# The first row pair's third outer product by seven inner products, and the second pair's partial results loaded in another order

## The chip, the cores and the metric

The kernel runs on one core of one Trainium2 chip. The metric is the device time of one execution in microseconds (us); lower is better.

## The reference

Soft routing over eight experts: every expert is applied to every token, and the results are added with the softmax of the router's logits as weights.

```
x: [16, 512, 512]   router_logits: [16, 512, 8]   expert_weights: [8, 512, 2048]   (float32)
probs  = softmax(router_logits, axis=-1)
output = sum over e of probs[:, :, e:e+1] * matmul(x, expert_weights[e])      # [16, 512, 2048]
```

For 8192 tokens this is one matrix product: its left factor is x scaled by each expert's probability (8192 rows, 8 x 512 = 4096 deep), its right factor the stacked expert weights (4096 x 2048).

## The kernel before

**Two levels of seven products.** The left factor is cut into 2x2 blocks (even and odd blocks of 256 rows; experts 0 to 3 and 4 to 7) and so is the right factor (the two halves of the experts; the two halves of 1024 columns: B11, B12, B21, B22). The 2x2 block product is done with seven outer products, P1 to P7, in Winograd's form. P1, P5, P2 and P4 come first, each in a stage of its own (`sub_product`), and their results are parked in DRAM tensors, `kept` for P1, P5 and P2, the output itself for P4. Each is split once more in the same way: seven *inner* products of half the size in place of eight. For that, the right factor of an outer product needs four *inner sums*, differences of its four blocks, each one VectorE subtraction over a tile `w` of 128x4096 (`inner_sums`): w5 (`sums[0]`), w6 (`sums[1]`, from w5), w4 (`sums[2]`, from w6) and w7 (`sums[3]`, which overwrites one block).

**The main loop.** The rest goes over 16 row pairs `q` (an even and an odd block of 256 rows each). A pair has four *quarters* (128 rows x 512 columns, `QUARTERS`). For every pair:

1. P6, plain: for each quarter, ScalarE copies the parked P1 (`m1`) into a PSUM bank (L626) and 16 matmuls of 128x512 add to it. VectorE then makes v = bank + parked P5 (`m5`). Between the quarters VectorE also does `c11` (parked P1 + parked P2 makes an output quarter) and `s4` (the left factor of P3), and `a11` for the following pair.
2. P7, plain: 16 more matmuls on each of the four banks. ScalarE copies each result out (`c21`, L664), VectorE adds m5 (`m5 = x + m5`), and GpSimd's queue writes both. VectorE makes the following pair's `s2` between them.
3. P3, whose right factor is B22 (tiles `w3`): in all pairs but the first by seven inner products on 128x512 quarters (`prod`, 7 x 8 matmuls), in the order P1, P2, P5, P6, P3, P7, P4. Inner P5 goes into a bank "q"; VectorE adds this bank to v11 (`r5`); then inner P3 accumulates into the same bank "q". VectorE also adds the bank "x" to v01 after inner P6, before inner P7 accumulates into it.

In the first pair, outer P3 is plain: 4 x 16 matmuls on banks seeded with v by ScalarE (`seeded`, L645), copied out by ScalarE (L681). B22's inner sums are made by VectorE at that time: w5, w6 and w4 during the first pair's P3, and w7, which overwrites a block that the plain P3 reads, in the second pair (`finish(sums)`). `rows.inner()` makes the four left sums of the inner products (VectorE, four operations on 128x8x128).

**What sets the order.** From the main loop on, VectorE and ScalarE work through their instructions in program order (`pinned`). The tile framework places the DMAs of SyncE (all loads of parked results and of x and probabilities) and of GpSimd (the writes of the main loop), and orders matmuls. Parked P1 and P2 tiles and the copied c21 share five buffers in rotation (`share(m=5, ...)`), parked P5 four (`v=4`), v four (`u=4`), r1 and r3 two. A load of a parked tile waits for the buffer's last user: for `m` an earlier output write, or the VectorE and ScalarE operations that read it.

`rows.load_kept(j)` loads the parked P1 and P5 of a quarter; `rows.c11(j)` loads P2 of the quarter and does the addition. `early(j)`, near the end of a pair, loads quarters 0 and 1 of the following pair, and does their `c11` unless it is the first pair's end: then the second pair does them itself, inside its P6.

Of the kernel before, what the change touches and what calls it, by code (L numbers as in the profile page):

```python
# [32 lines left out]
def kernel(  # L33
# [7 lines left out]
    nc = tc.nc  # L41
# [16 lines left out]
    NI = NHQ // 2  # L58
# [60 lines left out]
    act = dve  # L119

    def tt(o, a, b, op):
        dve(nc.vector.tensor_tensor(out=o, in0=a, in1=b, op=op))  # L122
# [15 lines left out]
    def bank():  # L138
        return psum.tile([P, NB], f32, name="ps", tag="ps")

    def mm(ps, z, w, start, stop):
        nc.tensor.matmul(ps, z, w, start=start, stop=stop, skip_group_check=True)  # L142
# [5 lines left out]
    def new_w():  # L148
        return wpool.tile([P, K8, NB], f16, name="w", tag="w")
# [23 lines left out]
    def inner_sums(b, t3=None):  # L173

        t3 = t3 or b[0, 1]
        w = {1: b[0, 0], 2: b[1, 0], 3: b[1, 1], 7: t3}

        def step(p, x, y):
            if p not in w:
                w[p] = new_w()  # L180
            tt(w[p], x, y, SUB)
        return w, [lambda: step(5, b[0, 1], b[0, 0]), lambda: step(6, b[1, 1], w[5]),
                   lambda: step(4, w[6], b[1, 0]), lambda: step(7, b[1, 1], b[0, 1])]

    def inner_weights(b):
        w, sums = inner_sums(b)
        sums[0]()
        yield
        sums[1]()
        sums[2]()  # L190
        yield
        sums[3]()
        return w
# [159 lines left out]
    def half(use="any"):  # L353
        return h_tile([P, NB], f32, use)

    def out_rows(i, odd, u, cols, n):
        return out_f[ds((2 * i + odd) * HQ + u * P, P), ds(cols * NH + n * NB, NB)]
# [72 lines left out]
    def finish(g):  # L430
        try:
            while True:
                next(g)
        except StopIteration as e:
            return e.value
# [6 lines left out]
    for n in range(2):  # L442
# [19 lines left out]
        if n == 0:  # L462
# [3 lines left out]
            w, sums = inner_sums(b11, new_w())  # L466
# [49 lines left out]
    w6, w7, w3 = {}, {}, {}  # L516
# [16 lines left out]
    QUARTERS = ((0, 0), (0, 1), (1, 1), (1, 0))  # L533

    class Rows:
# [57 lines left out]
        def put(self, odd, cols, tn, o, **how):  # L593
            queue = nc.sync if self.q == NI - 1 and not how else nc.gpsimd
            queue.dma_start(out=out_rows(self.q, odd, tn[0], cols, tn[1]), in_=o, **how)  # L595

    rows = Rows(0)
# [5 lines left out]
        rows.c11(j)  # L603
    pinned[0] = True
    o10 = None
    sums = inner_weights(w3)
    for q in range(NI):
        following = Rows(q + 1) if q + 1 < NI else None

        def ahead(make, k, following=following):  # L610
            if following:
                getattr(following, make)(k)

        def plain(ps, r, w, tn, start):
            t, n = tn
            for k in range(2 * K8):
                mm(ps, rows.z[r][k // K8][:, k % K8, ds(t * P, P)], w[k // K8, n][:, k % K8, :],
                   start, k == 2 * K8 - 1)


        xs, vs = [], []
        for j, tn in enumerate(QUARTERS):
            if j > 1:
                rows.load_kept(j)
            x = bank()
            act(nc.scalar.copy(x, rows.m1[tn]))  # L626
            if o10 and j == 0:
                o10()
            if j > 1 or q == 1:
                rows.c11(j)  # L630
            if j < 2:
                rows.s4(j)
            else:
                ahead("a11", j - 2)
            plain(x, 6, w6, tn, False)
            v = half("u")
            tt(v, x, rows.m5[tn], ADD)
            xs.append(x)
            vs.append(v)

        banks = {}

        def seeded(b, v, scale=1.0):
            banks[b] = bank()
            act(nc.scalar.mul(banks[b], v, scale))  # L645
        if q:
            seeded("b", vs[0])
            seeded("d", vs[3], -1.0)
            if q == NI - 1:
                seeded("e", vs[3], -1.0)  # L650
        else:
            seeded(0, vs[0])
            seeded(1, vs[1])


        if q == 1:
            inner3 = finish(sums)
        if q:
            z3 = rows.inner()
        for j, tn in enumerate(QUARTERS):  # L660
            x, m5 = xs[j], rows.m5[tn]
            plain(x, 7, w7, tn, False)
            c21 = half("m")
            act(nc.scalar.copy(c21, x))  # L664
            rows.put(1, 0, tn, c21, accum_op=ADD)
            tt(m5, x, m5, ADD)
            rows.put(1, 1, tn, m5)
            if j < 2:
                ahead("s2", j)


        def early(j):
            if following:
                following.load_kept(j)
                if q:
                    following.c11(j)

        ahead("s3", 0)
        if q == 0:
            def c12(j, tn, rows=rows, vs=vs, banks=banks):  # L680
                act(nc.scalar.copy(vs[j], banks[j]))  # L681
                rows.put(0, 1, tn, vs[j])

            for j, tn in enumerate(QUARTERS):
                plain(banks[j], 3, w3, tn, False)
                if j < 2:
                    seeded(j + 2, vs[j + 2])
                if j < 3:
                    c12(j, tn)
                if j < 2:  # L690
                    early(j)
                    next(sums)
            ahead("s3", 1)
            o10 = lambda: c12(3, QUARTERS[3])
            rows = following
            continue

        def prod(p, b):
            if b not in banks:
                banks[b] = bank()  # L700
            for k in range(K8):
                mm(banks[b], z3[p][:, k, :], inner3[p][:, k, :],
                   p in (1, 5) and k == 0, k == K8 - 1)
            return banks[b]

        def put(j, *args, rows=rows, vs=vs):
            tt(vs[j], *args)
            rows.put(0, 1, QUARTERS[j], vs[j])

        v00, v01, v11, v10 = vs  # L710
        x = prod(1, "x")
        r1 = half("r")
        act(nc.scalar.copy(r1, x))  # L713
        put(0, prod(2, "b"), r1, ADD)
        early(0)
        r5 = prod(5, "q")
        tt(v11, r5, v11, ADD)
        prod(6, "x")
        tt(v01, x, v01, ADD)
        early(1)  # L720
        put(1, prod(3, "q"), v01, ADD)
        prod(7, "x")
        r3 = half("r")
        act(nc.scalar.copy(r3, x))  # L724
        put(2, x, v11, ADD)
        ahead("s3", 1)
        if q < NI - 1:
            d = prod(4, "d")

            def o10(put=put, r3=r3, d=d):  # L730
                put(3, r3, d, SUB)
        rows = following
# [35 lines left out]
```

## Time and profile before

| | |
|---|---|
| median of 7 runs | 1434.1 us (1433.51 to 1436.21) |
| profiled execution: time / span | 1433.43 us / 1431.7 us |
| granted TensorE clock in the span | 1.000 |
| TensorE busy | 1424.8 us (100%), 6654 matmuls |
| VectorE busy | 1032.1 us (72%) |
| ScalarE busy | 271.4 us (19%) |
| GpSimd busy | 220.0 us (15%) |

The span goes from the first instruction's start to the last one's end; the profiled execution's time is 1.7 us longer. In a timeline, each line has a start, a duration, the engine, the source line, the operation, output and inputs, the shape and a count of merged instructions; in brackets stands how long the engine was idle before and what ended that. All VectorE additions and products of the main loop have line L122, all matmuls L142, all SyncE DMAs L133, the writes of outputs L595.

### The profile page before, as it was taken

How to read it: one execution, taken by the hardware profiler on the slowest of the kernel's cores; microseconds unless marked ns; L12 is line 12 of the kernel's file. 1: busy time of each engine (PE TensorE's matmuls, PEld its weight loads, DVE VectorE, ACT ScalarE, POOL GpSimd, SP SyncE). 2: the span in 40 equal slices, each digit the busy share in tenths (PEclk: the TensorE clock that was granted, in tenths of full speed). 3: DMA queues.
4: the chain of work that ended last, by engine and by line, in shares of the span. 5: the costliest groups of instructions: out<-in, count | busy, mean ns of one | idle time of the engine just before them, and what ended most of it. 6: DMA issues, size and time to landing. Idle time of an engine off the chain costs nothing.

```text
span 1431.7 us, 18172 instructions
## 1 busy us (share of the span) xinstructions
PE 1424.8 (100%) x6654; PEld 647.9 (45%) x6654; DVE 1032.1 (72%) x1173; ACT 271.4 (19%) x472; POOL 220.0 (15%) x344
## 2 busy tenths in 40 slices
PE   9999999999999999999999999999999999999998
PEld 4444444444444444444444444444444444444444
DVE  6967585656686867766767687777777877877773
ACT  3211111111111111111111211111111111111111
POOL 3111000110001000001000222222222222222220
PEclk9999999999999999999999999999999999999999
DMA  9899967899649994467866967787777767777764
GB/s 194 190 248 270 269 163 191 181 258 260 208 147 305 352 332 151 132 189 221 215 250 203 300 200 231 235 242 236 228 218 227 214 208 218 226 234 243 220 199 103
DMA packets 192041, 318.92 MB, mean 223 GB/s; under 512 B 51664, under 2 KB 80592, under 8 KB 187344
## 3 DMA queue, kind: packets, MB, share of 16 engines
q1 hardware_dynamic: 135328, 202.92, 44.5%
q0 software_dynamic: 56624, 114.84, 34.1%
q8 instruction: 52, 0.85, 0.2%
q14 instruction: 37, 0.30, 0.1%
HBM read 180.13 MB, written 159.58 MB: 237 GB/s over the span
## 4 chain that ended last, share of the span: by engine, by line
PE 93%; issue 3%; DMA 2%; POOL 1%; DVE 0%; ACT 0%; POOLq 0%; SPq 0%; DVEq 0%; ACTq 0%
PE ps L142 93%; POOL out_dram L595 1%; DMA out_dram<-h 1%; DMA w<-in_expert_weights_dram 0%; DMA h<-kept 0%; POOL w L136 0%; DVE z L122 0%; DVE h L122 0%; ACT ps L626 0%; SPq L133 0%; POOL ident L235 0%; POOLq L595 0%; DVEq L122 0%; POOLq L136 0%; POOLq L235 0%
## 5 line engine op out<-in xcount | busy, mean ns | idle before, releaser
L142 PE MATMUL ps<-w,z 128*128 128x512 f16 x6560 | 1415.2, 379 | 0.8 <-DMA w<-in_expert_weights_dram 0.4
L142 PEld LDWEIGHTS <-z 128*128 128x128 f16 x6560 | 641.6, 98 | 773.2 <-DVE z L122 1.1
L122 DVE TENSOR_TENSOR h<-ps,h 128x512 f32<-128x512 f32 x389 | 267.9, 689 | 313.6 <-PE ps L142 88.8
L122 DVE TENSOR_TENSOR z<-xT,pT 128x2048 f16<-128x2048 f16 x252 | 304.2, 1219 | 31.8 <-PE ps L142 31.2
L122 DVE TENSOR_TENSOR z<-z 128x2048 f16<-128x2048 f16 x280 | 303.6, 1108 | 7.3
L404 ACT COPY h<-ps 128x512 f32<-128x512 f32 x248 | 145.6, 587 | 601.8 <-PE ps L142 594.7
L595 POOL DMA_DIRECT2D out_dram<-h x244 | 154.1, 666 | 532.4 <-DVE h L122 324.7
L122 DVE TENSOR_TENSOR w<-w 128x4096 f16<-128x4096 f16 x36 | 82.3, 2286 | 0.9 <-DMA w<-wd 0.8
L664 ACT COPY h<-ps 128x512 f32<-128x512 f32 x64 | 37.5, 586 | 177.6 <-PE ps L142 176.0
L136 POOL DMA_DIRECT2D h<-in_x_dram x30 | 21.3, 711 | 263.7 <-DMA xT<-h 211.7
L122 DVE TENSOR_TENSOR h<-h,ps 128x512 f32<-128x512 f32 (+1 forms) x78 | 52.7, 676 | 11.0 <-PE ps L142 10.5
L122 DVE TENSOR_TENSOR h<-h 128x512 f32<-128x512 f32 (+1 forms) x67 | 46.0, 686 | 18.8 <-DMA h<-kept 18.7
L136 POOL DMA_DIRECT2D w<-in_expert_weights_dram x41 | 30.7, 763 | 186.4 <-DVE w L161 130.4
L645 ACT ACTIVATE ps<-h 128x512 f32<-128x512 f32 x35 | 21.0, 601 | 168.0 <-DVE h L122 168.0
L626 ACT COPY ps<-h 128x512 f32<-128x512 f32 x64 | 35.5, 592 | 32.6 <-DMA h<-kept 30.4
L136 POOL DMA_DIRECT2D w<-wd x12 | 6.5, 545 | 190.3 <-DVE w L161 116.5
L724 ACT COPY h<-ps 128x512 f32<-128x512 f32 x15 | 8.8, 587 | 120.7 <-PE ps L142 120.7
L713 ACT COPY h<-ps 128x512 f32<-128x512 f32 x15 | 8.8, 587 | 16.4 <-PE ps L142 16.4
L136 POOL DMA_DIRECT2D w<-wdt x8 | 4.4, 555 | 21.9 <-DVE w L161 21.9
L260 DVE CAST z<-ps 128x512 f16<-128x512 f32 x8 | 5.2, 686 | 3.5 <-PE ps L142 3.5
L260 DVE CAST xT<-ps 128x512 f16<-128x512 f32 x4 | 2.6, 687 | 5.4 <-PE ps L142 5.4
L142 PEld LDWEIGHTS <-w 128*128 128x128 f16 x80 | 5.0, 98 | 2.9 <-DMA w<-in_x_dram 1.5
(37 smaller groups left out, 44.2 us busy)
## 6 DMA issues: line engine op xcount, KB each, us to landing
out_dram<-h POOLq DMA_DIRECT2D x244, 256.0 KB, 4.9
kept<-h SPq DMA_DIRECT2D x192, 256.0 KB, 4.4
h<-kept SPq DMA_DIRECT2D x192, 256.0 KB, 4.5
pT<-p_dram SPq DMA_DIRECT2D x124, 256.0 KB, 5.0
w<-in_expert_weights_dram POOLq DMA_DIRECT2D x39, 512.0 KB, 12.9
out_dram<-h SPq DMA_DIRECT2D x75, 256.0 KB, 3.4
xT<-x SPq DMA_DIRECT2D x62, 256.0 KB, 2.9
w<-wd POOLq DMA_DIRECT2D x12, 1024.0 KB, 10.2
```

The lines of the kernel that those rows point to most:

```text
L122: dve(nc.vector.tensor_tensor(out=o, in0=a, in1=b, op=op))
L136: note(nc.gpsimd.dma_start(out=o, in_=i))
L142: nc.tensor.matmul(ps, z, w, start=start, stop=stop, skip_group_check=True)
L260: dve(nc.vector.tensor_copy(o, ps))
L404: nc.scalar.copy(t, ps)
L595: queue.dma_start(out=out_rows(self.q, odd, tn[0], cols, tn[1]), in_=o, **how)
L626: act(nc.scalar.copy(x, rows.m1[tn]))
L645: act(nc.scalar.mul(banks[b], v, scale))
L664: act(nc.scalar.copy(c21, x))
L713: act(nc.scalar.copy(r1, x))
L724: act(nc.scalar.copy(r3, x))
```

## The change

In the first pair, outer P3 is done by seven inner products like in all others. `rows.inner()` and the seeding of banks "b" and "d" are now also done there, and the four inner sums of B22 stand in the first pair: w5 before `rows.inner()`, w6 after the first quarter of P7, w7 after the fourth quarter of P7, w4 after inner P2. The following pair's `s2` parts move from quarters 0 and 1 of P7 to quarters 1 and 2, its first `s3` part from ahead of the inner products to after inner P3. In the second pair, the parked P1 and P5 of quarters 2 and 3 are loaded at the start of P6, ahead of the P2 loads of `c11`.

```diff
-    sums = inner_weights(w3)
+    inner3, sums = inner_sums(w3)
...
-            if j > 1:
+            if j > 1 and q != 1:
                 rows.load_kept(j)
+            if q == 1 and j == 0:
+                rows.load_kept(2)
+                rows.load_kept(3)
...
-        if q:
-            seeded("b", vs[0])
-            seeded("d", vs[3], -1.0)
-            if q == NI - 1:
-                seeded("e", vs[3], -1.0)
-        else:
-            seeded(0, vs[0])
-            seeded(1, vs[1])
+        seeded("b", vs[0])
+        seeded("d", vs[3], -1.0)
+        if q == NI - 1:
+            seeded("e", vs[3], -1.0)
...
-        if q == 1:
-            inner3 = finish(sums)
-        if q:
-            z3 = rows.inner()
+        if q == 0:
+            sums[0]()
+        z3 = rows.inner()
...
-            if j < 2:
-                ahead("s2", j)
+            if q:
+                if j < 2:
+                    ahead("s2", j)
+            elif j < 3:
+                (lambda: sums[1](), lambda: ahead("s2", 0), lambda: ahead("s2", 1))[j]()
...
-        ahead("s3", 0)
-        if q == 0:
-            def c12(j, tn, rows=rows, vs=vs, banks=banks):
-                act(nc.scalar.copy(vs[j], banks[j]))
-                rows.put(0, 1, tn, vs[j])
-
-            for j, tn in enumerate(QUARTERS):
-                plain(banks[j], 3, w3, tn, False)
-                if j < 2:
-                    seeded(j + 2, vs[j + 2])
-                if j < 3:
-                    c12(j, tn)
-                if j < 2:
-                    early(j)
-                    next(sums)
-            ahead("s3", 1)
-            o10 = lambda: c12(3, QUARTERS[3])
-            rows = following
-            continue
+        if q:
+            ahead("s3", 0)
+        else:
+            sums[3]()
...
         put(0, prod(2, "b"), r1, ADD)
         early(0)
+        if q == 0:
+            sums[2]()
         r5 = prod(5, "q")
         tt(v11, r5, v11, ADD)
         prod(6, "x")
         tt(v01, x, v01, ADD)
         early(1)
         put(1, prod(3, "q"), v01, ADD)
+        if q == 0:
+            ahead("s3", 0)
```

## Prediction

> **What bounds the kernel.** I read the page first: busy times and the chain that ended last.
>
> ```profile
> span 1431.7 us, 18172 instructions
> ...
> PE 1424.8 (100%) x6654; PEld 647.9 (45%) x6654; DVE 1032.1 (72%) x1173; ACT 271.4 (19%) x472; POOL 220.0 (15%) x344
> ...
> PE 93%; issue 3%; DMA 2%; POOL 1%; DVE 0%; ACT 0%; POOLq 0%; SPq 0%; DVEq 0%; ACTq 0%
> ```
>
> TensorE is the bound. A matmul less is worth its interval; an operation elsewhere costs nothing until TensorE waits for it. Next, the chain of waits in order of time, around the second pair:
>
> ```profile
> 837.32 4.23 DMA h<-kept
> ...
> 841.63 0.60 ACT ps L626
> 842.23 0.04 issue
> 842.27 585.53 PE ps L142 x2720
> ```
>
> After 842.27 there is no gap: 585.53/2720 = 0.2153 us per matmul. Just before it, the second pair's fourth P6 quarter waited for its parked P1, loaded last. The timeline's line for the weight loads gives the size of this wait:
>
> ```profile
> 842.27 62.69 PEld L142 LDWEIGHTS <-z 128*128 128x128 f16 x291 [0.33 <-issue]
> ```
>
> Without a wait that idle time is 0.215 - 0.097 = 0.12 us, so TensorE lost 0.21 us. These are the places where the change acts. VectorE's timeline there (first pair, end of P6 to P3):
>
> ```profile
> 803.56 0.69 DVE L122 TENSOR_TENSOR h<-h 128x512 f32<-128x512 f32 x1 [4.46 <-DMA h<-kept]
> ...
> 807.67 1.36 DVE L122 TENSOR_TENSOR h<-ps,h 128x512 f32<-128x512 f32 x2
> 808.95 1.22 DVE L122 TENSOR_TENSOR z<-xT,pT 128x2048 f16<-128x2048 f16 x1
> 810.20 1.23 DVE L122 TENSOR_TENSOR z<-z 128x2048 f16<-128x2048 f16 x1
> ...
> 818.75 0.69 DVE L122 TENSOR_TENSOR h<-ps,h 128x512 f32<-128x512 f32 x1 [2.81 <-ACT h L664]
> ...
> 821.75 6.94 DVE L122 TENSOR_TENSOR w<-w 128x4096 f16<-128x4096 f16 x3
> 828.60 1.22 DVE L122 TENSOR_TENSOR z<-xT,pT 128x2048 f16<-128x2048 f16 x1
> ```
>
> VectorE comes late into P7: a parked tile kept it idle until 803.56, and the fourth v is made only at 807.67 (the first of the merged two). ScalarE shows when P7's fourth quarter ended, 818.13:
>
> ```profile
> 818.13 0.59 ACT L664 COPY h<-ps 128x512 f32<-128x512 f32 x1 [2.91 <-PE ps L142]
> ```
>
> **Matmuls.** 64 become 56: 8 x 0.2153 = 1.72 us less. All of it is on the path.
>
> **VectorE, where the gain goes.** The first pair gets the four sums before its inner products need them, four left sums, and six additions. In the order of the changed kernel's instructions, from the fourth v to the r5 addition, each stands behind the one before. Costs are start to start: an addition 0.60 to 0.61 (rows above); a sum 2.19 where the next operation does not read it (2.28 long, the next starts 0.09 before its end); the s2 part of one k 1.25 + 1.15 = 2.40 (808.95, 810.20, and then the next could start at 811.35); the four left sums 2.66, from this row in the second pair, whose successor starts at 851.44:
>
> ```profile
> 848.78 2.74 DVE L122 TENSOR_TENSOR z<-z 128x1024 f16<-128x1024 f16 x4
> ```
>
> 807.67 + v 0.61 + w5 2.19 + left sums 2.66 + m5 0.61 + w6 2.19 + m5 0.60 + s2 2.40 + m5 0.60 + s2 2.40 + m5 0.60 + w7 2.19 + put of P2 0.60 + w4 2.19 = 827.51: r5 starts, ends 0.69 later, 828.20. No other engine holds this chain up: the fourth m5 addition would start at 821.9 (its bank is ready at 818.7) and the P2 addition at 824.7 (P2 is ready at 818.13 + 2 x 1.72 = 821.6). So VectorE is saturated for 20 us.
>
> TensorE does inner P1, P2, P5 and P6 from P7 on without a wait (w5 is there at 810.5, w6 at 816.0): P6's results are seen at 818.13 + 4 x 1.72 = 825.0, and the next matmul could start some 0.2 us before that, at 824.8. Two instructions wait there. In the changed order one inner P4 matmul stands ahead of P3, and it needs w4 (827.6); P3 accumulates into bank "q", so it needs r5 to have read it (828.2). In other pairs r5 costs nothing, since VectorE waits for TensorE, as in the third:
>
> ```profile
> 904.63 0.69 DVE L122 TENSOR_TENSOR h<-ps,h 128x512 f32<-128x512 f32 x1 [0.24 <-PE ps L142]
> ```
>
> With 0.05 us from one engine to the other (ScalarE's end 842.22, matmul 842.27), P3 starts at 828.25 where it could at 824.8: 3.45 us, less the 0.22 of the P4 matmul done in it. **Stall: +3.23 us.** Behind the waiting matmul on TensorE stand P3, P7, P4 and all of the second pair. Its size hangs on the start, 807.67, which DMAs set; I allow 0.8 us either way. P7 needs the x addition, at 828.8, and w7, at 824.8: no further wait.
>
> **B22 itself.** The sums now start at 808.3. Do the blocks land in time?
>
> ```profile
> L136 POOL DMA_DIRECT2D w<-wd x4: 531/536/551, 780.4 to 785.5; - x4
> ...
> DMA to landing us min/median/max: 6.8/10.2/12.5
> ```
>
> At the latest at 785.5 + 12.5 = 798.0; 10 us of cover. Nothing.
>
> **ScalarE, GpSimd, SyncE.** ScalarE loses four seeds and four copies, gains two of each: about 2.4 us less on an engine that is 19% busy. Seed "d" waits for the fourth v (808.36), so the first c21 copy goes from 807.7 to about 809; the m5 additions go later by about 4 us (the first from 808.3 to 813.1), and so do their output writes, and behind them on GpSimd's queue the later c21 writes. These writes free the buffers for the second pair's loads, which issue on SyncE from 814 to 829 and are read by ScalarE from 832 on: hidden.
>
> **The second pair's loads.** All four parked P1 are there by about 829, the seeds come in time, and the 0.21 us wait of before goes: **-0.21 us**. In return the five `m` buffers now hold P1, and the P2 loads of quarters 1 to 3 each wait for the previous quarter's `c11` to free one: addition, issue, landing, addition. VectorE is in order, so s4, the v additions and a11 wait behind each. How long is a landing there?
>
> ```profile
> L133 SPq DMA_DIRECT2D h<-kept x4: 320/320/372, 831.7 to 846.8; - x4
> ...
> DMA to landing us min/median/max: 2.6/3.7/4.4
> ```
>
> The first c11 ends at about 837.5; each following one starts one landing and about 0.8 us after the last. With 3.7 us the fourth starts at 837.6 + 3 x 3.7 + 1.6 = 850.3. From there to the end of the second pair's r5 are 16.6 us of VectorE work by the same prices (a11, v, left sums, four m5, two s2, s3, two additions, r5): 866.9. TensorE, at the second pair's P6 from 833.2 (828.25 + 23 matmuls), would start that inner P3 at 833.2 + 128 x 0.2153 + 32 x 0.2153 = 867.7. Fits, with 0.8 us to spare; landings of 4.0 us would use it up. I take zero; at 4.4 us each (the row's end) it costs about 1.3, at 4.7 about 2.2. Not below zero: nothing there waits in before.
>
> **Clock.** TensorE would stand still for some 3 us with one matmul in between. Nothing in this trace idles it so long after the start; only the first matmuls ran at the slow rate (634 against 379 ns long; nine intervals from 1.3 to 5.1 us are 0.42 each, 0.21 over the normal 0.2153, 1.9 us in all):
>
> ```profile
> L104 PE MATMUL every<-h x10: 531/634/634, 1.3 to 5.1; 128*128 128x512 f16 x10
> ```
>
> So the bounds are 0 and 1.9 us; I take 0, since the page's row of the granted clock has full speed in all slices. [...]
>
> **Sum.** -1.72 + 3.23 - 0.21 = **+1.30 us** on the profiled execution: 1433.43 + 1.30 = 1434.7. The median of the runs is 0.7 us above that execution, so I forecast 1435.4 (+0.09%). A measurement of this kernel can tell about 0.2%, 2.9 us, from no change: this lies within.
>
> **Rivals.**
>
> *No stall (chance 0.12).* If VectorE had the fourth v at about 804.3 (P6's end) in place of 807.67, r5 would end at 824.8 and the whole saving would stay: -1.72 - 0.21 = -1.9, 1432.2 us. Against it: the late parked tiles are loaded before the change begins, by the same queue in the same order. More than 1.93 us can't be gained, so faster by over 0.2% needs a cause that I don't see.
>
> *The P2 loads in series (0.15).* If the landings take more than 4.0 us each, VectorE carries its lateness through the second pair and TensorE waits a second time, at that pair's inner P3. At 4.5 us, the median of all such loads on the page, three landings are 2.4 us longer than at 3.7, 0.8 of which is cover: +1.6, so +2.9 and 1437.0 us; at 4.7, 1437.6. It decides from 4.5 us on. For it: that median. Against it: here they go out one at a time, where the trace's landings are short.
>
> *The clock falls (0.05).* The stall takes it to half, up to +1.9: +3.2, 1437.3 us.
>
> The forecast keeps 0.68. That the change doesn't act can be excluded: the changed order has 8 matmuls fewer.
>
> **Range and chances.** The forecast's own range is 1434.4 to 1436.6 (start of the chain, partial waits in the second pair). With the two slow rivals up to 1437.8, and down to 1432.6, which leaves out the rival without a stall and the outermost cases. Slower by over 0.2%: most of the two slow rivals and little else, 0.17. Faster: 0.02. Within: 0.81.
>
> **What would show it.** In the changed profile: TensorE waits for VectorE (a line w or h) once in the first pair, near 827.6, for about 3 us; VectorE has no idle time from about 804 to 828; the wait at 842 is gone; the second pair's third c11 or fourth shows a wait for DMA, and its r5 does or does not follow TensorE. Wrong if no such stall stands there, if r5 ends by 825, or if the time differs from before by over 2.9 us.

## The result and the profile after

| | before | changed |
|---|---|---|
| median | 1433.79 us (31 runs, 1432.9 to 1438.03) | 1438.42 us (13 runs, 1434.6 to 1440.15) |
| profiled execution: time / span | 1433.43 / 1431.7 us | 1435.12 / 1433.4 us |
| matmuls | 6654 | 6646 |

The ratio is 1.0027, 95% interval [1.0019, 1.0034]: slower by 0.27%, 4.6 us. The forecast was 1435.4 us, in a range of 1432.6 to 1437.8: the direction and the place are as predicted, the size is not. The profiled execution is the second quickest of the 13; other profiles of the changed kernel follow below.

The page of the changed kernel, the lines that answer to those shown of before, and the group of the matmuls:

```profile
span 1433.4 us, 18150 instructions
...
PE 1424.5 (99%) x6646; PEld 647.5 (45%) x6646; DVE 1037.0 (72%) x1183; ACT 268.6 (19%) x468; POOL 219.8 (15%) x344
...
PE 94%; DMA 3%; DVE 2%; issue 0%; SPq 0%; POOL 0%; DVEq 0%; POOLq 0%
...
L142 PE MATMUL ps<-w,z 128*128 128x512 f16 x6552 | 1415.3, 379 | 2.7 <-DVE w L122 1.8
```

Eight matmuls fewer, and yet the busy time of this group is what it was (1415.2 us before): some matmuls took longer. VectorE has come into the chain. TensorE's timeline shows where it waits, first pair, inner P6 to P3:

```profile
814.76 9.88 PE L142 MATMUL ps<-w,z 128*128 128x512 f16 x45
826.45 0.38 PE L142 MATMUL ps<-w,z 128*128 128x512 f16 x1 [1.81 <-DVE w L122]
827.05 13.29 PE L142 MATMUL ps<-w,z 128*128 128x512 f16 x53 [0.23 <-DVE h L122]
```

The single matmul is P4's first: it waits for w4 (a tile w). P3 behind it waits for r5 (h). Start to start the two waits are 2.19 and 0.60 us in place of 0.2157 each: 2.36 us lost. VectorE meanwhile, from the end of P6:

```profile
802.39 0.69 DVE L122 TENSOR_TENSOR h<-h 128x512 f32<-128x512 f32 x1 [4.65 <-DMA h<-kept]
...
806.48 0.68 DVE L122 TENSOR_TENSOR h<-ps,h 128x512 f32<-128x512 f32 x1
807.08 2.28 DVE L122 TENSOR_TENSOR w<-w 128x4096 f16<-128x4096 f16 x1
...
824.12 2.28 DVE L122 TENSOR_TENSOR w<-w 128x4096 f16<-128x4096 f16 x1
826.32 1.28 DVE L122 TENSOR_TENSOR h<-ps,h 128x512 f32<-128x512 f32 x2
```

No bracket between 802.39 and 826.32: VectorE is saturated. From the fourth v (806.48) to r5 (826.32) it takes 19.84 us, as the prediction added up.

The windows of the changed kernel give busy time by engine (TensorE first) and then, after GpSimd's, the granted clock:

```profile
820.00:823.40 3.40, 3.40 (x18) 1.51 (x16) 3.40 (x3) 0.09 (x1) 0.71 (x2) 1.00 1.09 236
823.70:827.10 3.40, 1.36 (x7) 0.45 (x6) 3.40 (x4) 0.00 (x0) 0.54 (x1) 1.00 1.00 280
827.10:830.50 3.40, 3.40 (x9) 1.22 (x9) 0.50 (x1) 0.00 (x0) 0.00 (x0) 0.50 0.91 325
830.50:833.90 3.40, 3.40 (x17) 1.50 (x16) 3.23 (x4) 1.51 (x3) 0.54 (x1) 1.00 0.29 111
```

In the third stretch the clock is at half, and 9 matmuls are counted where 17 are in the fourth. That is the second loss. It is not peculiar to this execution: over the whole span the mean granted clock is 0.997 to 0.999 in 12 of the 13 runs and 1.000 in the quickest alone; in the runs of before that were measured beside the experiments it is 1.000 in 53 of 61. From the end of P7 (817.57, where inner P1's first matmul starts) to the second pair's first matmul (833.70) are 16.13 us; 56 matmuls at 0.2157 are 12.08, the waits 2.36, and the rest, 1.69, the halved clock.

### The profile page after: what moved, and what is told of

It is laid out like the page before. It is cut to its first block, busy times and chain, and to the rows that moved or that the text cites. A ratio compares the mean times of both kernels' runs of the same rounds, so it can differ in the third digit from the quotient of the medians.

```text
span 1433.4 us, 18150 instructions
## 1 busy us (share of the span) xinstructions
PE 1424.5 (99%) x6646; PEld 647.5 (45%) x6646; DVE 1037.0 (72%) x1183; ACT 268.6 (19%) x468; POOL 219.8 (15%) x344
## 4 chain that ended last, share of the span: by engine, by line
PE 94%; DMA 3%; DVE 2%; issue 0%; SPq 0%; POOL 0%; DVEq 0%; POOLq 0%
PE ps L142 94%; DMA out_dram<-h 2%; DVE z L122 1%; DVE w L122 1%; DVE h L122 1%; DMA w<-in_expert_weights_dram 0%; DMA h<-kept 0%; SPq L133 0%; POOL w L136 0%; POOL ident L235 0%; DVEq L122 0%; POOLq L235 0%; POOLq L742 0%
## 5 line engine op out<-in xcount | busy, mean ns | idle before, releaser
L122 DVE TENSOR_TENSOR h<-ps,h 128x512 f32<-128x512 f32 x394 | 270.9, 688 | 304.0 <-PE ps L142 95.4
L122 DVE TENSOR_TENSOR z<-z 128x2048 f16<-128x2048 f16 (+1 forms) x284 | 306.3, 1102 | 7.4
L122 DVE TENSOR_TENSOR h<-h,ps 128x512 f32<-128x512 f32 (+1 forms) x79 | 53.4, 675 | 11.1 <-PE ps L142 10.2
## 6 DMA issues: line engine op xcount, KB each, us to landing
w<-wd POOLq DMA_DIRECT2D x12, 1024.0 KB, 10.2
```

## The experiments

Theory A: VectorE is late in the first pair, TensorE waits for it before inner P3, and the clock falls. Rival B: the second pair's P2 loads, one behind the other, make TensorE wait there. Rival C: the time is lost bit by bit later.

**The changed kernel again, three profiles.** No edit.

> The changed kernel once more, unaltered, for a profile of one of its usual executions (most took 1437 to 1440 us; the one profiled took 1435.1). Theory A (VectorE is late in the first pair): TensorE waits about 2 to 3.5 us near 827 and then runs one stretch of 3.4 us at half clock, which costs 1.7 us; the larger times come from a longer wait there and from a second half-clock stretch directly behind it. Rival B (the P2 loads of the second pair go in series): the larger times show a second wait of 1 to 4 us at inner P3 of the second pair, near 868, and a half-clock stretch behind that one. Rival C (lost bit by bit in later pairs): no wait over 0.5 us after 832, and the sum of small ones is 3 us or more.

> The changed kernel again, for another profile. Theory A alone: one wait near 827 to 830 of 2 to 5 us with half clock behind it, none in the second pair over 0.5 us. With rival B: a second wait near 868 to 872, of 1 to 4 us, in an execution of 1438 us or more, with a second half-clock stretch.

> The same once more, for how the start of VectorE's chain (the fourth v of the first pair, 806.5 to 809.6 us in the profiles so far) and the wait in the first pair go together: by theory A each microsecond that the fourth v comes later makes the wait one microsecond longer.

The first of them had 1438.21 us (8 runs; ratio 1.0027 [1.0017, 1.0037]). All four profiles of the changed kernel side by side; the wait is the sum of both intervals over 0.2157:

| profile | time | fourth v starts | P7 ends | wait | at half clock | lost by it |
|---|---|---|---|---|---|---|
| changed | 1435.12 | 806.48 | 817.57 | 2.36 | 3.41 | 1.69 |
| e18_again | 1436.83 | 808.51 | 817.68 | 4.29 | 3.41 | 1.34 |
| e1_again | 1438.09 | 809.55 | 817.99 | 5.02 | 3.41 | 1.28 |
| e19_again | 1438.69 | 809.77 | 818.12 | 5.11 | 6.83 | 1.93 |

(All in us; the last column is worked out as above. The mean granted clock over the span is 0.999 in the first three and 0.998 in e19_again.) A fourth v that comes 1 us later against P7's end makes the wait 1 us longer: -11.09 gives 2.36, -9.17 gives 4.29, -8.35 gives 5.11. That is theory A's line, and nothing is fitted in it. Behind the first pair almost nothing is lost: the second pair takes 39.7 us (184 matmuls) in three of the four, and 0.27 more in e1_again; from there to the end TensorE has no gap in any of them. B and C fall for this kernel as it stands. Why the fourth v comes late is seen on VectorE, first line of e1_again, second of e19_again, the line that stands at 803.56 before:

```profile
805.47 0.69 DVE L122 TENSOR_TENSOR h<-h 128x512 f32<-128x512 f32 x1 [5.78 <-DMA h<-kept]
```

```profile
805.69 0.69 DVE L122 TENSOR_TENSOR h<-h 128x512 f32<-128x512 f32 x1 [6.39 <-DMA h<-kept]
```

A parked tile lands up to 3.3 us later than in the changed kernel's first profile (802.39).

**The first pair alone**, the second pair's loads as before.

```diff
-            if j > 1 and q != 1:
+            if j > 1:
                 rows.load_kept(j)
-            if q == 1 and j == 0:
-                rows.load_kept(2)
-                rows.load_kept(3)
```

> The first pair's seven inner products alone: the second pair loads parked P1 and P5 in the order of before. Theory A: the wait near 827 stays as it is (2 to 3.5 us), and the wait for the fourth parked P1 of the second pair comes back and is longer than before's 0.2 us, since the loads now start later: 1 to 4 us near 847. Time 1438 to 1442 us, slower than the changed kernel or like it. Rival B: without the loads in series the second pair loses nothing, time about 1435.5 us, faster than the changed kernel by 2 us or more.

1442.96 us (5 runs; ratio 1.0054 [1.0041, 1.0068]), 4.5 us above the changed kernel. TensorE's timeline, from the longest of the five (1444.69 us):

```profile
829.28 17.61 PE L142 MATMUL ps<-w,z 128*128 128x512 f16 x73 [3.75 <-DVE w L122]
851.21 49.14 PE L142 MATMUL ps<-w,z 128*128 128x512 f16 x215 [4.32 <-ACT ps L626]
```

The second wait is the seed of the second pair's fourth P6 quarter: the parked P1 loaded last. It was 0.2 us before and is 4.5 now, with a half-clock stretch of its own. The buffers come free later behind the busier VectorE: in the chain of this profile the load starts at 847.36, once an output write that started at 840.69 has landed; before, the write started at 831.98 and the load at 837.32. So the new load order is not a small gain beside the main change but what keeps the main change from costing twice as much.

**The load order alone**, first pair plain.

```diff
-            if j > 1:
+            if j > 1 and q != 1:
                 rows.load_kept(j)
+            if q == 1 and j == 0:
+                rows.load_kept(2)
+                rows.load_kept(3)
```

> The new load order of the second pair alone: the first pair's P3 stays plain, with 64 matmuls. Theory A: the wait of 0.2 us at 842 goes and nothing comes for it, since VectorE is on time in the first pair: 0.2 to 0.7 us less than before (1433.2 us). Rival B: VectorE waits for three P2 loads one after the other and TensorE for VectorE at inner P3 of the second pair: 1.5 us or more slower than before.

1433.48 us (11 runs) against 1433.80; ratio 0.9997 [0.9988, 1.0006]: no difference to be measured. In its profile TensorE has one unbroken stretch from before 803 to 880, so the wait of 0.2 us is gone and nothing replaces it. And its fourth v starts at 809.52, as late as in e1_again, at no cost: with plain P3 no matmul of the first pair waits for VectorE.

**w4 later.**

```diff
-        if q == 0:
-            sums[2]()
         r5 = prod(5, "q")
         tt(v11, r5, v11, ADD)
         prod(6, "x")
         tt(v01, x, v01, ADD)
+        if q == 0:
+            sums[2]()
```

> The changed kernel with the sum w4 moved from ahead of the r5 addition to behind the addition that follows inner P6; everything else as changed. Theory A: r5 ends 2.2 us earlier, the wait of TensorE in the first pair falls from 2 to 3.4 us to 0 to 1.2 us, the clock stays full there, and the time falls by 2.2 us for the wait and 1.7 us for the clock: about 1434.5 us. If only the wait matters and not the clock: about 1436. Rival B: the first pair's wait is not what makes the larger times, and the time stays within 1 us of the changed kernel, with the wait at inner P3 of the second pair.

1435.72 us (11 runs; ratio 1.0010 [1.0002, 1.0019]): 2.7 us won. The profile is of an execution of 1434.32 us:

```profile
827.39 72.98 PE L142 MATMUL ps<-w,z 128*128 128x512 f16 x336 [2.39 <-DVE h L122]
```

The fourth v started at 809.03, the wait is 2.56 us (0.2 more than the table's line gives with w4's 2.19 off), and the clock stayed full in this execution (1.000 over the span). The mechanism holds. The expected 1434.5 was too low: the start was again taken from the earliest profile, and in other executions the clock seems to have fallen even so (its mean over the span is 0.997 in the longest, 1438.34 us, and 1.000 in five of the eleven).

**w4 and half of s2 later.** As the one before, and:

```diff
-            elif j < 3:
-                (lambda: sums[1](), lambda: ahead("s2", 0), lambda: ahead("s2", 1))[j]()
+            elif j < 2:
+                (lambda: sums[1](), lambda: ahead("s2", 0))[j]()
...
         put(1, prod(3, "q"), v01, ADD)
         if q == 0:
+            ahead("s2", 1)
             ahead("s3", 0)
```

> The changed kernel with w4 behind the addition after inner P6 (as in the run before) and with the second half of the following pair's s2 moved from P7's third quarter to behind inner P3's output: 4.6 us of VectorE work less ahead of r5. Theory A (only VectorE's lateness in the first pair costs): no wait over 0.7 us in the first pair, clock full, 1432 us. Theory A with rival B (the P2 loads of the second pair go in series and cost by themselves): no wait in the first pair, but 0.5 to 3 us at inner P3 of the second pair, near 866, and 1433 to 1436 us.

1437.52 us (6 runs; ratio 1.0026 [1.0015, 1.0038]). Nothing is left of the gain, though the first pair's wait is gone entirely in the profile (1439.33 us, the longest of the six):

```profile
809.76 38.15 PE L142 MATMUL ps<-w,z 128*128 128x512 f16 x176
848.10 7.07 PE L142 MATMUL ps<-w,z 128*128 128x512 f16 x32 [0.19 <-DVE h L122]
855.63 10.52 PE L142 MATMUL ps<-w,z 128*128 128x512 f16 x48 [0.46 <-DVE h L122]
869.66 30.52 PE L142 MATMUL ps<-w,z 128*128 128x512 f16 x128 [3.51 <-DVE h L122]
```

Rival B's wait, at inner P3 of the second pair, and the clock at half for 6.83 us behind it (its mean over the span is 0.998): the pair takes 47.09 us in place of 39.69. VectorE in this execution waits for the P2 loads:

```profile
844.37 0.69 DVE L122 TENSOR_TENSOR h<-h 128x512 f32<-128x512 f32 x1 [3.40 <-DMA h<-kept]
...
853.15 0.69 DVE L122 TENSOR_TENSOR h<-h 128x512 f32<-128x512 f32 x1 [2.67 <-DMA h<-kept]
```

The changed kernel has such waits too (2.17 and 2.60 us, at 843.07 and 851.70); there TensorE is later by its own loss and does not notice them.

**And the first c11 of the second pair at the end of the first.** As the one before, and:

```diff
-            if j > 1 or q == 1:
+            if j > 1 or q == 1 and j == 1:
                 rows.c11(j)
...
         put(2, x, v11, ADD)
+        if q == 0:
+            following.c11(0)
         ahead("s3", 1)
```

> The one before, and in addition the P2 load and addition of the second pair's first quarter stand at the end of the first pair, so that only two of the P2 loads follow one another inside the second pair's P6 (the chain starts some 4 us earlier). Theory A with rival B: both waits are gone (under 0.7 us each), the clock stays full, and the 1.7 us of the eight matmuls come through: 1431.7 to 1432.5 us, 0.1% less than before the change. If rival B is not at work: the same time as the one before.

1432.15 us (11 runs; ratio 0.9989 [0.9980, 0.9997]): faster than before the change. In its profile (1433.17 us) one wait is left, of 1.61 us at inner P3 of the first pair; the second pair has none:

```profile
826.42 73.76 PE L142 MATMUL ps<-w,z 128*128 128x512 f16 x341 [1.45 <-DMA out_dram<-h]
```

The profile names an output write as what ended the wait. But r5 ends at 826.37, 0.05 us before, the same distance as in e4_w4_later, where VectorE is named; so I take it to be r5 here too, after a fourth v as late as 810.44. The expectation allowed 0.7.

**And w5 and w6 inside P6.** As the one before, and `sums[0]` behind the second quarter's s4, `sums[1]` at the start of the third quarter:

```diff
+            if q == 0 and j == 2:
+                sums[1]()
             x = bank()
...
                 rows.s4(j)
+                if q == 0 and j == 1:
+                    sums[0]()
...
-        if q == 0:
-            sums[0]()
         z3 = rows.inner()
...
-            elif j < 2:
-                (lambda: sums[1](), lambda: ahead("s2", 0))[j]()
+            elif j == 1:
+                ahead("s2", 0)
```

> As the one before, and w5 and w6 are made inside the first pair's P6, where VectorE waits for parked tiles (once 1.4 and once 4.5 us in the profile of before): a further 4.4 us of VectorE work less after the fourth v. Theory A: nothing is left to win in the first pair if the one before has no wait there: same time, 1431.7 to 1432.5 us, and less spread of the times if late parked tiles still made some executions wait. Rival: the sums in P6 delay the c11 additions and v, and P7 waits for v: 1 us or more slower than the one before.

1431.77 us (11 runs, 1431.05 to 1432.37; ratio 0.9986 [0.9976, 0.9995]). VectorE now makes the two sums where it waited for the parked tile:

```profile
796.49 2.29 DVE L122 TENSOR_TENSOR w<-w 128x4096 f16<-128x4096 f16 x1
...
799.29 2.28 DVE L122 TENSOR_TENSOR w<-w 128x4096 f16<-128x4096 f16 x1
805.13 0.69 DVE L122 TENSOR_TENSOR h<-h 128x512 f32<-128x512 f32 x1 [3.56 <-DMA h<-kept]
```

```profile
809.69 90.60 PE L142 MATMUL ps<-w,z 128*128 128x512 f16 x419
```

In this profile, which is of the quickest run, TensorE runs without a gap through both pairs. The median is 2.2 us less than before, for 1.72 + 0.21 expected. Against e8_c110 it is 0.4 us, which the two intervals don't tell apart; its longest run is 0.9 us below e8_c110's longest. This is the version to keep.

**The wait filled with matmuls.**

```diff
         early(1)
+        if q == 0:
+            fill = bank()
+            for k in range(14):
+                mm(fill, z3[1][:, 0, :], inner3[1][:, 0, :], True, True)
         put(1, prod(3, "q"), v01, ADD)
```

> The changed kernel with 14 needless matmuls of 128x512 (3.0 us) into a spare bank between inner P6 and inner P3 of the first pair, where TensorE waits for VectorE; the output is untouched. If the halved clock is a cost of its own beside the wait: TensorE doesn't stand still long enough, the clock stays full in that place, and the time is 1 to 1.7 us less than the changed kernel's (about 1436.8 us) although 14 matmuls more run. If the wait alone costs, or the clock's fall is hidden: the same time as the changed kernel, 1438.2 us. If the wait were shorter than 3 us: up to 1 us slower.

1437.68 us (6 runs; ratio 1.0030 [1.0019, 1.0042]): by time alone not to be told from the changed kernel. The profile says more:

```profile
829.31 39.87 PE L142 MATMUL ps<-w,z 128*128 128x512 f16 x184 [1.31 <-DVE h L122]
870.14 30.16 PE L142 MATMUL ps<-w,z 128*128 128x512 f16 x139 [0.96 <-DVE h L122]
```

The clock stayed full in this execution (over the span its mean is 1.000 in four of the six runs and 0.999 in two). From P7's end to the second pair 16.58 us, against 17.71 in e18_again, whose fourth v lies as far ahead of P7's end (9.17 us), and that with 14 matmuls more: the clock is a loss of its own, over 1 us here. But the second pair, reached earlier, then waits 1.13 us for VectorE, and gives it back.

**The changed kernel with c11(0) early, alone.** The edit of e8_c110 on the changed kernel.

> The changed kernel with one alteration: the P2 load and addition of the second pair's first quarter stand at the end of the first pair. VectorE's lateness in the first pair is untouched. If the P2 loads in series cost something in the changed kernel's usual executions (rival B beside theory A): the wait in the first pair stays at 2 to 4.6 us, no wait at inner P3 of the second pair, and the time falls by 0.5 to 2 us, to about 1437 us, with less time at half clock. If the first pair's wait is the whole loss: 1438.2 us as the changed kernel.

1437.81 us (9 runs; ratio 1.0025 [1.0015, 1.0035]): no gain that can be told from none. In its profile the wait in the first pair is 4.12 us (fourth v 808.53), the granted clock has a mean of 0.997 over the span, and the second pair takes 39.72 us, as in three of the four profiles above. So B costs nothing that can be seen in the changed kernel; it is the next limit once A is out of the way.

## Why the prediction was right and where it failed

**Matmuls, -1.72 us: right.** 56 matmuls stand on the path; where nothing waits (e15_all) the gain arrives.

**The wait, +3.23 us: right in place, cause and slope, wrong in size.** The two matmuls named wait for the two operations named, and the price list from fourth v to r5 is met (19.84 us). What was mis-sized is the start: 807.67, taken from one execution of before, with 0.8 us either way. In the profiles it lies between 806.5 and 810.4, mostly near 809; three of the four waits are 4.3 to 5.1. Given its start, the forecast was met: 807.67 is 10.2 us ahead of P7's end in the profile of before (817.88), for which the table's line gives 3.3 us. Before the change this spread has no price (e3_loads_only: 809.52, and no wait), so one profile of before gave no hint that its value was an early one.

**The clock, 0: wrong.** It fell in all four profiles of the changed kernel, 1.3 to 1.9 us each. I gave the case 0.05. The 0 was my estimate, from a profile of before in which the clock is full in all slices and nothing idles TensorE so long after the start; of the runs, e4_w4_later shows it (2.56 us of waiting, clock full), the four profiles of the changed kernel the opposite. The rival's price (up to 1.9) came out by luck: it counts the nine slow matmuls at the kernel's start, while 3.41 us at half clock hold eight of 0.427 us, and e5_spread, with 6.83 us at half clock, lost 2.7. In the changed kernel's profile the clock fell at 827.1 after 1.98 and 0.39 us of waiting with a matmul in between, and TensorE was at work for 1.36 of the 3.40 us before.

**The sum.** For e1_again: -1.72 + 5.02 + 1.28 - 0.21 + 0.27 = +4.6 us. The medians differ by 4.6. For the other three profiles (the changed kernel's first, e18_again, e19_again) the terms give +2.1, +3.7 and +5.1. P7 ends 0.3 us earlier, 0.2 earlier and 0.2 later there than in the profile of before; with that, +1.8, +3.5 and +5.3, where their times differ from that of before by +1.7, +3.4 and +5.3. What is left unnamed is about 0.1 us. By the prediction's own signs, the stall, its place and r5's end (827.0) held, and the time failed: it differs by more than 2.9 us, a case that was given 0.17.

**The second pair: right as far as it went.** The 0.21 us wait is gone. The P2 loads in series cost nothing here (0.27 us at most, in e1_again), as I took it, but the cover was not the one that I named (0.8 us of slack in VectorE): TensorE's own loss covers them. Without that loss they cost 4.7 us of waiting (3.67 of it at inner P3) and 2.7 of clock (e5_spread).

**ScalarE, GpSimd, B22's landing: right.** None of them ends a wait of TensorE in the changed kernel. The second pair's loads were issued from 808.8 to 828.8 and waited for by no seed; e2_first_only shows that this needs the new order.

The rival without a stall, 1432.2, is what e8_c110 and e15_all reach, by shortening what stands ahead of r5 and by starting the second pair's P2 loads earlier.

## What to carry to other kernels

An engine with slack on average (VectorE, 72% busy) may have none in the stretch where new work is put: add up its chain up to the first operation that the bound engine needs, and take the chain's start from several executions, since a start that is hidden now varies at no cost and shows its spread only when something depends on it. Put new work where that engine waits for a DMA, and what the bound engine needs soonest ahead of what is only needed later. When a wait is removed and the time doesn't move, look for the wait behind it before the idea is given up: here two had to go together.

## What the runs showed of the hardware

A wait of TensorE of 2.4 us in two parts (the changed kernel's profile) was enough to halve the clock once; unbroken waits of 2.56 (e4_w4_later) and 1.61 us (e8_c110) were not, in the executions profiled (1.000 over the span in both). The half-clock stretches were 3.41 us long (the changed kernel's profile) or 6.83 (e19_again), and did not all begin at the wait's end: in e19_again the clock fell at 827.5, 2.3 us before the waiting matmul started, and stayed at half until 834.3:

```profile
823.70:827.10 3.40, 1.49 (x7) 0.59 (x6) 3.40 (x4) 0.00 (x0) 0.56 (x1) 1.00 1.10 264
827.50:830.90 3.40, 1.13 (x3) 0.36 (x3) 3.40 (x3) 0.00 (x0) 0.54 (x1) 0.50 1.03 344
830.90:834.30 3.40, 3.40 (x10) 1.21 (x8) 0.34 (x1) 0.00 (x0) 0.00 (x0) 0.50 0.74 283
```

So the length of the wait alone does not say whether the clock falls, and TensorE's share of work just ahead does not either. In the 3.40 us up to the fall it was at work for 1.36 us (40%) in the changed kernel (823.70 to 827.10), and for 1.09 us (32%) in e19_again, where its matmuls ended at 825.19. In e4_w4_later it was at work for 1.01 of the 3.40 us up to 827.39 (30%), and the clock stayed full. What decides was not shown: no run singles it out.

The chain of waits of the changed kernel's profile leads back to the boundary of the stages:

```profile
785.42 12.46 DMA out_dram<-h
...
798.83 3.44 DMA h<-kept
```

A write of 256 KB took 12.46 us there, beside the loads of B22's four blocks of 1024 KB (issued from 780 to 786), where the page's median for such writes is 3.6. The parked tile's load stands behind it on SyncE. Moving B22's loads was not tried. The write alone does not make the spread of the fourth v: in e18_again and e19_again it ends at 797.97 and 799.17, near to the 797.88 here. What differs more is the parked tile's own load. It was issued at 798.8 here, 798.9 in e18_again, 800.3 in e1_again and 800.1 in e19_again, and took 3.4, 5.4, 5.0 and 5.5 us to land. In the profile of before it took 3.5, in e3_loads_only 5.4. So the one profile that the prediction took its start from had, by chance, a quick landing; why landings differ by 2 us between executions stays open.
